# A row softmax on one core: row maxima leave the main path, ten tiles become five, and one queue carries every transfer

## The chip, the cores and the metric

The kernel runs on one core of a Trainium2 chip. The metric is the device time of one execution in microseconds (us), the median of several runs.

## The reference, cut to what matters

```python
# x: (16, 1024, 512) float32, drawn from a standard normal distribution
x_scaled = x / 2.0
x_max = np.max(x_scaled, axis=-1, keepdims=True)
exp_x = np.exp(x_scaled - x_max)
return (exp_x / np.sum(exp_x, axis=-1, keepdims=True)).astype(np.float32)
```

Each of the 16,384 rows of 512 numbers is normalised on its own. Subtracting the row maximum leaves the quotient as it is as long as neither the exponentials nor their sum leave the range of float32.

## The kernel before

Spread over 128 partitions, the 16,384 rows are 128 rows for each partition, and "a row" below means one row in every partition: 128 x 512 floats, 262,144 bytes. The table PLAN cuts the 128 rows into ten tiles of 3, 7, 13 and seven times 15 rows. A tile is what one load and one store move. In DRAM, the rows of a tile that belong to one partition lie next to each other, so a tile of 15 rows moves 30,720 contiguous bytes for each partition. Tiles are cut further into chunks of 3 to 5 rows, 27 in all, which is what the engines work on.

The data lies in one SBUF buffer, `arena`, with room for 98 of the 128 rows. Each tile is computed in place. The last two tiles (8 and 9) reuse the places of tiles 0 to 3, so their loads (L190) must wait until the stores of those tiles have landed.

For each chunk the work passes through three steps:

- VectorE takes the negated row maxima into `stats` (`reduce_max`, L118). It first waits for the tile's load.
- ScalarE computes exp(0.5 x + bias) with the negated maximum as bias, one `activation` per row, and writes the sum of the row over the maximum in `stats` (L176 in straight code, L211 in a loop). The bias is the maximum of the unscaled row, a different shift from that of the reference; the quotient is the same.
- VectorE takes the reciprocal of the sums (L127) and multiplies the chunk by it: as one broadcast multiply over the chunk for tiles 1 to 3 (L131), as one multiply for each row in the other tiles (L138).

VectorE's order is written by hand: the maximum of chunk k stands before the reciprocal and multiply of chunk k - 2 (LAG is 2). ScalarE's order is straight code for tiles 0 to 5. For tiles 6 to 9 it is a loop over chunks of 5 rows (L201 to L220) with addresses taken from a register. The loop waits at L203 on a semaphore `s_go` that TensorE's sequencer raises for it (L168), since TensorE has nothing else to do.

There are two transfer queues. SyncE's queue issues the load of tile 0 and then all ten stores in order, each once the last multiply of its tile is done (L158). ScalarE's queue issues all other loads: tile 1 in three pieces (L110), tiles 2 to 7 (L114), and tiles 8 and 9 (L190) from within the straight code of its exponentials. The first loads are moved ahead of the barrier at the program's start. The program ends when SyncE has seen the last stores land (L162).

Of the kernel before, what the change touches and what calls it, by code (L numbers as in the profile page):

```python
# [6 lines left out]

PLAN = [
    ([3], 0), ([4, 3], 3), ([5, 4, 4], 10), ([5] * 3, 23), ([5] * 3, 38), ([5] * 3, 53),
    ([5] * 3, 68), ([5] * 3, 83), ([5] * 3, 0), ([5] * 3, 15),
]
ARENA = 98
LAG = 2

SPREAD = 1

AFTER = {8: 4, 9: 5}  # L20

FUSED = {1, 2, 3}

LOOP = 6
E = 5


@with_exitstack
def kernel(
# [5 lines left out]
    nc = tc.nc  # L35
    tc.close()
    tc.compile()
    fp32 = mybir.dt.float32

    xf = x.flatten_outer_dims()  # L40
    of = out.flatten_outer_dims()
    N, D = xf.shape
    P = nc.NUM_PARTITIONS
    n_rows = N // P
    assert sum(sum(c) for c, _ in PLAN) == n_rows

    arena = nc.alloc_sbuf_tensor("arena", (P, ARENA, D), fp32)

    stats = nc.alloc_sbuf_tensor("stats", (P, n_rows), fp32)
    recip = nc.alloc_sbuf_tensor("recip", (P, n_rows), fp32)  # L50

    tiles, chunks, base = [], [], 0
    for t, (cs, at) in enumerate(PLAN):
        r = sum(cs)
        tiles.append((base, r, at))
        o = 0
        for c in cs:
            chunks.append((t, base + o, c, at + o))  # L60
            o += c
        base += r
    last_chunk = {c[0]: k for k, c in enumerate(chunks)}

    def dram(ap, t):
        b, r, _ = tiles[t]
        return ap[b * P : (b + r) * P].rearrange("(p r) d -> p r d", r=r)

    def sb(t):
        _, r, at = tiles[t]  # L70
        return arena[:, at : at + r, :]


    behind = {}
    for t, (_, r, at) in enumerate(tiles):
        for u in range(t):
            _, ru, au = tiles[u]
            if at < au + ru and au < at + r:
                behind.setdefault(t, []).append(u)

    ld = [nc.alloc_semaphore(f"ld{t}") for t in range(len(tiles))]
    awaited = sorted({u for us in behind.values() for u in us})


    st, need = {}, {}
    for t in sorted(behind):
        new = [u for u in behind[t] if u not in st]
        sem = nc.alloc_semaphore(f"st{t}")
        st.update({u: sem for u in new})
        need[t] = (sem, 16 * len(new))  # L90
    s_end = nc.alloc_semaphore("s_end")
    s_max = nc.alloc_semaphore("s_max")
    s_exp = nc.alloc_semaphore("s_exp")
    s_go = nc.alloc_semaphore("s_go")
    s_rec = nc.alloc_semaphore("s_rec")
    s_mul = nc.alloc_semaphore("s_mul")

    def issue_loads(begin, end):


        for t in range(begin, end):
            if t in behind:
                continue
            if t == 0:
                nc.sync.dma_start(out=sb(t), in_=dram(xf, t)).then_inc(ld[t], 16)
            elif t == SPREAD:

                r = tiles[t][1] - 1
                for p, q, lo, hi in ((0, P, 0, r), (0, 126, r, r + 1), (126, P, r, r + 1)):
                    nc.scalar.dma_start(  # L110
                        out=sb(t)[p:q, lo:hi], in_=dram(xf, t)[p:q, lo:hi]
                    ).then_inc(ld[t], 16)
            else:
                nc.scalar.dma_start(out=sb(t), in_=dram(xf, t)).then_inc(ld[t], 16)  # L114

    def do_max(k):
        t, b, c, a = chunks[k]
        nc.vector.reduce_max(  # L118
            out=stats[:, b : b + c],
            in_=arena[:, a : a + c],  # L120
            axis=mybir.AxisListType.X,
            negate=True,
        )._wait_ge(ld[t], 48 if t == SPREAD else 16).then_inc(s_max, 1)

    def do_mul(k):
        t, b, c, a = chunks[k]
        nc.vector.reciprocal(  # L127
            out=recip[:, b : b + c], in_=stats[:, b : b + c]
        )._wait_ge(s_exp, k + 1).then_inc(s_rec, 1)
        if t in FUSED:  # L130
            nc.vector.tensor_mul(  # L131
                out=arena[:, a : a + c],
                in0=arena[:, a : a + c],
                in1=recip[:, b : b + c].unsqueeze(2).to_broadcast([P, c, D]),
            )._wait_ge(s_rec, k + 1).then_inc(s_mul, 1)
            return
        for r in range(c):
            ins = nc.vector.tensor_scalar_mul(  # L138
                out=arena[:, a + r],
                in0=arena[:, a + r],  # L140
                scalar1=recip[:, b + r : b + r + 1],
            )
            if r == 0:
                ins._wait_ge(s_rec, k + 1)
        ins.then_inc(s_mul, 1)

    def compute_and_store():

        for k in range(len(chunks) + LAG):
            if k < len(chunks):  # L150
                do_max(k)
            if k >= LAG:
                do_mul(k - LAG)


        for t in range(len(tiles)):
            nc.sync.wait_ge(s_mul, last_chunk[t] + 1)
            nc.sync.dma_start(out=dram(of, t), in_=sb(t)).then_inc(  # L158
                st[t] if t in awaited else s_end, 16
            )  # L160

        nc.sync.wait_ge(s_end, 16 * (len(tiles) - len(awaited)))  # L162


        straight = [k for k, c in enumerate(chunks) if c[0] < LOOP]
        loop = [k for k, c in enumerate(chunks) if c[0] >= LOOP]
        for k in loop:
            nc.tensor.wait_ge(s_max, k + 1).then_inc(s_go, 1)  # L168


        nc.scalar.preload_act_table(mybir.ActivationFunctionType.Exp)  # L171
        late = sorted(behind)
        for k in straight:
            t, b, c, a = chunks[k]
            for r in range(c):
                ins = nc.scalar.activation(  # L176
                    out=arena[:, a + r],
                    in_=arena[:, a + r],
                    func=mybir.ActivationFunctionType.Exp,
                    bias=stats[:, b + r : b + r + 1],  # L180
                    scale=0.5,
                    accum_out=stats[:, b + r : b + r + 1],
                )
                if r == 0:
                    ins._wait_ge(s_max, k + 1)
            ins.then_inc(s_exp, 1)
            while late and last_chunk[AFTER[late[0]]] <= k:
                u = late.pop(0)
                nc.scalar.wait_ge(*need[u])
                nc.scalar.dma_start(out=sb(u), in_=dram(xf, u)).then_inc(ld[u], 16)  # L190
        assert not late


        first = chunks[loop[0]][1]
        assert all(
            c == E and b == first + j * E and a == b % ARENA
            for j, (_, b, c, a) in enumerate(chunks[k] for k in loop)
        )
        row = nc.scalar.alloc_register("row")
        nc.scalar.reg_mov(row, first)  # L200
        with nc.scalar.While(lambda: nc.scalar.snap(row, min_val=first, max_val=n_rows) < n_rows):  # L201
            now = nc.scalar.snap(row, min_val=first, max_val=n_rows - E)
            nc.scalar.wait_ge(s_go, 1).then_inc(s_go, -1)  # L203
            at = nc.s_assert_within(
                now % ARENA, 0, ARENA - E,
                skip_runtime_bounds_check_because="no chunk reaches over the arena's end",
            )
            for r in range(E):
                data = arena[:, r : ARENA - E + 1 + r][:, bass.ds(at, 1)]
                stat = stats[:, r : n_rows - E + 1 + r][:, bass.ds(now, 1)]  # L210
                ins = nc.scalar.activation(  # L211
                    out=data,
                    in_=data,
                    func=mybir.ActivationFunctionType.Exp,
                    bias=stat,
                    scale=0.5,
                    accum_out=stat,
                )
            ins.then_inc(s_exp, 1)
            nc.scalar.reg_add(row, row, E)  # L220

    here = str(nc.cur_bb)
    entry, rest = nc.main_func.blocks[0], list(nc.main_func.blocks[1:])
    head, jumps = entry.instructions[:-5], entry.instructions[-5:]
    entry.instructions = []
    nc.switch_bb("main", None)
    issue_loads(0, 2)
    first = list(entry.instructions)  # L230
    at = next(k for k, i in enumerate(head) if type(i).__name__ == "InstDrain")
    entry.instructions = head[:at] + first + head[at:]
    act = []
    entry.instructions = list(entry.instructions) + [i for i in jumps if i not in act]
    nc.switch_body(here, parent=None, valid_engines=[i.engine for i in jumps])
    issue_loads(2, len(tiles))
    compute_and_store()


# [28 lines left out]
```

## Time and profile before

| what | value |
|---|---|
| median of 3 runs | 160.08 us (160.05 to 160.23) |
| profiled execution, its own time | 160.0 us |
| its span in the profile | 158.6 us |
| VectorE busy | 131.4 us, 83% of the span |
| ScalarE busy | 94.4 us, 60% of the span |
| TensorE | only waits and signals, no busy time |
| read from and written to HBM | 33.55 MB each, 423 GB/s over the span |
| transfer packets | 3026, of them 336 under 2 KB |

The span is the time from the first to the last instruction that the profiler recorded; the execution's own time is 1.4 us longer. The page counts an engine as busy only while it computes. The row "DMA" is the mean busy share of the core's 16 transfer engines in each of 40 equal slices of the span, and "GB/s" is what they moved in that slice. Queue q1 is SyncE's and q10 is ScalarE's; q14 fetches instructions. "ACTq" and "SPq" are the sequencers of ScalarE and SyncE, which handle registers, branches, waits and transfer issues; "ACT" and "DVE" are the engines ScalarE and VectorE.

### The profile page before, as it was taken

Reading aid. Unit: us, or ns where it says so; the run is one execution under the profiler, and the core shown is the slowest. Engines: PE = TensorE matmul, PEld = TensorE weight load, DVE = VectorE, ACT = ScalarE, POOL = GpSimd, SP = SyncE. Lnnn points to the kernel's source line nnn. Section 1 sums busy time; section 2 is a strip of 40 time slices with the busy share of each in tenths; the row PEclk is TensorE's granted clock in tenths of the full one; section 3 lists DMA queues with packets and bytes.
Section 4 is the critical chain, followed back from the end, with each engine's and each line's share of the span. In section 5 each row is a group of like instructions: output and inputs, shape, how many; then the busy total and the mean of one; then the engine's idle time right before and its main releaser. Section 6 shows DMA issues by size and latency. Waiting matters only on the chain.

```text
span 158.6 us, 621 instructions
## 1 busy us (share of the span) xinstructions
DVE 131.4 (83%) x155; ACT 94.4 (60%) x257; POOL 0.2 (0%) x4
## 2 busy tenths in 40 slices
DVE  0466799999999999999999999996999389999000
ACT  0369197736874594669738797666566809763000
POOL 0000000000000000000000000000000000000000
DMA  7999999999999999999999999999999999999996
GB/s 268 449 373 430 414 431 466 435 407 399 466 443 389 434 463 448 418 444 426 442 426 434 426 426 442 426 441 411 457 395 472 395 473 395 472 395 465 395 472 263
DMA packets 3026, 67.13 MB, mean 423 GB/s; under 512 B 336, under 2 KB 336, under 8 KB 720
## 3 DMA queue, kind: packets, MB, share of 16 engines
q1 hardware_dynamic: 1584, 34.34, 50.6%
q10 hardware_dynamic: 1440, 32.77, 48.5%
q14 instruction: 2, 0.02, 0.0%
HBM read 33.55 MB, written 33.55 MB: 423 GB/s over the span
## 4 chain that ended last, share of the span: by engine, by line
DMA 52%; DVE 38%; issue 0%
DMA arena<-in_x_dram 38%; DVE stats L118 18%; DMA out_dram<-arena 14%; DVE arena L131 13%; DVE arena L138 7%; DVE recip L127 1%
## 5 line engine op out<-in xcount | busy, mean ns | idle before, releaser
L118 DVE TENSOR_REDUCE stats<-arena 128x5 f32<-128x2560 f32 (+2 forms) x27 | 72.2, 2676 | 14.6 <-DMA arena<-in_x_dram 14.6
L176 ACT ACTIVATE arena<-arena,stats 128x512 f32<-128x512 f32 x68 | 48.2, 710 | 23.4 <-DVE stats L118 23.4
L211 ACT ACTIVATE arena<-arena,stats x60 | 42.5, 710 | 20.7 <-ACTq L203 20.7
L138 DVE TENSOR_SCALAR arena<-arena,recip 128x512 f32<-128x512 f32 x93 | 38.6, 482 | 0.7
L131 DVE TENSOR_TENSOR arena<-arena,recip 128x2560 f32<-128x2560 f32 (+2 forms) x8 | 19.9, 2491 | 0.3
L176 ACT ACTIVATION_READ_ACCUMULATOR arena<-arena,stats 128x1 f32 x68 | 12.7, 187 | 0.0
L211 ACT ACTIVATION_READ_ACCUMULATOR arena<-arena,stats x60 | 11.2, 187 | 0.0
L127 DVE RECIPROCAL recip<-stats 128x5 f32<-128x5 f32 (+2 forms) x27 | 4.8, 177 | 0.0
L171 ACT ACT_TABLE_LOAD x1 | 1.3, 1283 | 5.7 <-issue 5.7
L252 POOL MEMSET const-bfloat16-1.0<- 128x1 bf16 x1 | 0.1, 101 | 0.0
L252 POOL MEMSET const-uint8-127<- 128x1 uint8 x1 | 0.1, 101 | 0.0
L252 POOL MEMSET const-float32-0.0<- 128x1 f32 x1 | 0.1, 98 | 0.2 <-issue 0.2
L252 POOL MEMSET const-float32-1.0<- 128x1 f32 x1 | 0.1, 98 | 0.0
## 6 DMA issues: line engine op xcount, KB each, us to landing
arena<-in_x_dram ACTq DMA_DIRECT2D x7, 3840.0 KB, 46.6
out_dram<-arena SPq DMA_DIRECT2D x7, 3840.0 KB, 22.7
arena<-in_x_dram ACTq DMA_DIRECT2D x1, 3328.0 KB, 14.3
out_dram<-arena SPq DMA_DIRECT2D x1, 3328.0 KB, 21.1
out_dram<-arena SPq DMA_DIRECT2D x1, 1792.0 KB, 18.2
arena<-in_x_dram ACTq DMA_DIRECT2D x1, 1536.0 KB
arena<-in_x_dram SPq DMA_DIRECT2D x1, 768.0 KB, 6.2
out_dram<-arena SPq DMA_DIRECT2D x1, 768.0 KB, 15.8
```

Source lines behind the costliest of these rows:

```text
L118: nc.vector.reduce_max(out=stats[:, b : b + c], in_=arena[:, a : a + c], axis=mybir.AxisListType.X, negate=True,)._wait_ge(ld[t], 48 if t ...
L127: nc.vector.reciprocal(out=recip[:, b : b + c], in_=stats[:, b : b + c])._wait_ge(s_exp, k + 1).then_inc(s_rec, 1)
L131: nc.vector.tensor_mul(out=arena[:, a : a + c], in0=arena[:, a : a + c], in1=recip[:, b : b + c].unsqueeze(2).to_broadcast([P, c, D]),)._w ...
L138: ins = nc.vector.tensor_scalar_mul(out=arena[:, a + r], in0=arena[:, a + r], scalar1=recip[:, b + r : b + r + 1],)
L171: nc.scalar.preload_act_table(mybir.ActivationFunctionType.Exp)
L176: ins = nc.scalar.activation(out=arena[:, a + r], in_=arena[:, a + r], func=mybir.ActivationFunctionType.Exp, bias=stats[:, b + r : b + r ...
L211: ins = nc.scalar.activation(out=data, in_=data, func=mybir.ActivationFunctionType.Exp, bias=stat, scale=0.5, accum_out=stat,)
L252: nc = _bacc.Bacc("TRN2", target_bir_lowering=False, num_devices=1)
```

## The change

The change does six things at once.

- **No row maxima on the main path.** ScalarE computes exp(0.5 x) without a bias and sums each row. VectorE only takes reciprocals and multiplies.
- **A check of the sums and a general path.** At the end VectorE counts, for each partition, the sums that lie between 1.0 and 1e30. TensorE adds the 128 counts with one matmul, and VectorE turns the total into a flag. VectorE, ScalarE and SyncE each read the flag into a register. Where it says that every sum was in range, they skip a loop; otherwise the loop does the whole softmax again in 16 tiles of 8 rows with row maxima.
- **Five tiles** of 30, 30, 30, 25 and 13 rows instead of ten. A tile of 30 rows moves 61,440 contiguous bytes for each partition. Tiles 3 and 4 reuse the place of tile 0.
- **All transfers on SyncE's queue**, in this order: load 0 (ahead of the barrier), loads 1 and 2, store 0, store 1, then a wait until store 0 has landed, loads 3 and 4, stores 2, 3 and 4. ScalarE issues none.
- **ScalarE loops from the start**: 25 rounds of 5 rows, then 3 rows in straight code. TensorE raises `s_go` when a tile's load has landed, by the number of chunks in the tile.
- **One broadcast multiply for every chunk** (25 of 5 rows, one of 3) in place of 93 multiplies of single rows and 8 broadcast ones. The hand-written alternation with the maxima is gone.

Line numbers in the changed kernel: transfers are issued at L93 (loads) and L97 (stores), reciprocals at L127, multiplies at L130, the loop's exponentials at L237 and the last three at L163, the check at L135 to L145, the matmul at L154, the reading of the flag at L110.

```diff
-PLAN = [
-    ([3], 0), ([4, 3], 3), ([5, 4, 4], 10), ([5] * 3, 23), ([5] * 3, 38), ([5] * 3, 53),
-    ([5] * 3, 68), ([5] * 3, 83), ([5] * 3, 0), ([5] * 3, 15),
-]
+TILES = [(30, 8), (30, 38), (30, 68), (25, 0), (13, 25)]
...
+    def load(eng, t):
+        eng.dma_start(out=sb(t), in_=dram(xf, t)).then_inc(ld[t], 16)
+
+    def store(t):
+        nc.sync.wait_ge(s_mul, upto[t])
+        nc.sync.dma_start(out=dram(of, t), in_=sb(t)).then_inc(
+            s_first if t == 0 else s_end, 16
+        )
+
+    def take(eng, sem, n):
+        eng.wait_ge(sem, n).then_inc(sem, -n)
+
+    def rounds(eng, body):
+        last = n_rows // G
+        i = eng.alloc_register("tile")
+        eng.wait_ge(s_flag, 1)
+        eng.reg_load(i, flag[0:1, 0:1])
+        with eng.While(lambda: eng.snap(i, min_val=0, max_val=last) < last):
+            body(eng.snap(i, min_val=0, max_val=last - 1))
+            eng.reg_add(i, i, 1)
...
+        for k, (b, c) in enumerate(zip(starts, sizes)):
+            a = (b + SHIFT) % ARENA
+            nc.vector.reciprocal(
+                out=recip[:, b : b + c], in_=stats[:, b : b + c]
+            )._wait_ge(s_exp, k + 1).then_inc(s_rec, 1)
             nc.vector.tensor_mul(
                 out=arena[:, a : a + c],
                 in0=arena[:, a : a + c],
                 in1=recip[:, b : b + c].unsqueeze(2).to_broadcast([P, c, D]),
             )._wait_ge(s_rec, k + 1).then_inc(s_mul, 1)
...
+        for t in range(len(tiles)):
+            nc.tensor.wait_ge(ld[t], 16).then_inc(s_go, owner.count(t))
+        nc.tensor.wait_ge(s_ones, 1)
+        nc.tensor.matmul(
+            total[:, :], lhsT=count[:, :], rhs=ones[:, :], start=True, stop=True
+        )._wait_ge(s_cnt, 3).then_inc(s_tot, 1)
+
+        nc.scalar.preload_act_table(Exp)
+        exponentials(0, n_rows - LAST)
...
+        store(0)
+        store(1)
+        nc.sync.wait_ge(s_first, 16)
+        load(nc.sync, 3)
+        load(nc.sync, 4)
+        for t in range(2, len(tiles)):
+            store(t)
...
+        rounds(nc.vector, vector)
+        rounds(nc.scalar, scalar)
+        rounds(nc.sync, sync)
+        nc.sync.wait_ge(s_end, 16 * (len(tiles) - 1))
...
+            take(nc.scalar, s_go, 1)
             at = nc.s_assert_within(
-                now % ARENA, 0, ARENA - E,
+                (now + SHIFT) % ARENA, 0, ARENA - E,
...
                 ins = nc.scalar.activation(
-                    out=data,
-                    in_=data,
-                    func=mybir.ActivationFunctionType.Exp,
-                    bias=stat,
-                    scale=0.5,
-                    accum_out=stat,
+                    out=data, in_=data, func=Exp, scale=0.5,
+                    accum_out=stats[:, r : n_rows - E + 1 + r][:, bass.ds(now, 1)],
                 )
```

## The prediction, made before the changed kernel ran

> **What bounds the kernel now.** I read the transfers first, since the same bytes must move after the change. The page's slices and queue rows:
>
> ```profile
> DVE  0466799999999999999999999996999389999000
> ACT  0369197736874594669738797666566809763000
> ...
> DMA  7999999999999999999999999999999999999996
> ...
> q1 hardware_dynamic: 1584, 34.34, 50.6%
> q10 hardware_dynamic: 1440, 32.77, 48.5%
> ```
>
> The transfer engines are full from the first slice to the last; the two queues add up to 99.1% of them. VectorE has three empty slices at the end and ScalarE gaps all along, so neither sets the end. Next, stretches of the span (DVE, ACT and POOL busy, clock, DMA share, GB/s): only loads, mixed, and only stores on SyncE's queue:
>
> ```profile
> 6.20:14.60 8.40, 7.04 (x7) 6.06 (x16) 0.00 (x0) 1.00 1.06 426
> 80.00:127.00 47.00, 42.64 (x63) 32.72 (x90) 0.00 (x0) 1.00 1.01 433
> 127.00:157.00 30.00, 19.11 (x33) 10.91 (x30) 0.00 (x0) 1.00 1.00 433
> ```
>
> The three rates agree: neither the direction nor the number of queues matters, and one queue alone holds 433 GB/s. So the time is transfer work plus every gap in it. The work is in the packet records: a 30,720-byte packet takes 1.138 us (median), a 26,624-byte one 0.987, 14,336 0.535, 6,144 0.234; each engine has 8 packets per full tile. Ten tiles make 8 x (7 x 1.138 + 0.987 + 0.535 + 0.234) = 77.8 us each way, 155.6 in both; the split of tile 1 and 9-ns semaphore packets bring 155.8. Engines begin between 1.0 and 1.8 us and end with the last store at 157.5 to 158.2, so some 0.7 us is lost, mostly before 10 us, where first packets run slow (0.4 to 0.8 us instead of 0.234).
>
> For the edges I read ScalarE's and VectorE's timeline. The page's groups first:
>
> ```profile
> L118 DVE TENSOR_REDUCE stats<-arena 128x5 f32<-128x2560 f32 (+2 forms) x27 | 72.2, 2676 | 14.6 <-DMA arena<-in_x_dram 14.6
> L211 ACT ACTIVATE arena<-arena,stats x60 | 42.5, 710 | 20.7 <-ACTq L203 20.7
> ```
>
> The maxima cost VectorE 72.2 us, and ScalarE's loop waits 20.7 us for them through L203. What a loop round itself costs is hidden in that wait; the sequencer's own rows show it, for the round whose activations run from 82.39 to 86.02 us:
>
> ```profile
> L220 ACTq ALU_OP  x1: 44/44/44, 83.1 to 83.1; - x1
> L201 ACTq COMPARE_BRANCH  x2: 38/42/45, 83.2 to 83.4; - x2
> L203 ACTq EVENT_SEMAPHORE  x1: 17/17/17, 86.3 to 86.3; - x1
> ```
>
> Addition and branch run at 83.1 to 83.4, with three rows still to compute. Only L203's wait held the next round, until the maximum ended at 86.15; the next activation began at 86.51, 0.36 us later. With `s_go` raised in advance a round should cost five rows and nothing more.
>
> **What the Trainium skill says.** *DMA: Bandwidth & Descriptors*, "Issuing engines are not separate DMA queues": transfers of all issuers interleave on the same 16 engines. The trace agrees: one queue gives 433 GB/s, as two do. "Where 436 GB/s comes from" has a ceiling of 435.2 GB/s; 433 stands on it, so rate can't be won. *Advanced Engine Details and Errata*, "Engine Queue Depths": ScalarE holds 8 queued instructions; the early branch agrees with a queue ahead of the engine. "Latency and other measured facts" of the first page prices a `tensor_load` at about 600 ns; no run shows it yet.
>
> **Transfer work after the change.** From 26,624 to 30,720 bytes a packet grows by 0.0369 ns a byte; I carry that on: 61,440 bytes 2.271 us, 51,200 1.893. Each way 8 x (3 x 2.271 + 1.893 + 0.987) = 77.5 us, both ways 155.1, with semaphores 155.2: 0.6 less than before. No record exceeds 30,720 bytes; bounds: -0.1 us if fixed cost per packet vanishes, +3 us if large packets run 2% slower. I take the line. The start loses the slow first packets once more, but no second queue joins; I take half of the 0.7 us back, between none and all.
>
> **Whether a gap opens.** In queue order, slowest engine, 18.17 us for 30 rows: load 0 begins at 1.8, with 0.5 for the slow first packet, and lands at 20.4; load 1 at 38.6, load 2 at 56.7; store 0 at 74.9, store 1 at 93.1, load 3 at 108.2, load 4 at 116.1, store 2 at 134.3, store 3 at 149.4, store 4 at 157.3. Fast engines are 0.7 us ahead. An issue has to come before its predecessor ends there.
>
> Compute: from landing through TensorE's signal to the first activation 0.36 (semaphore packet at 127.30, VectorE at 127.66) plus the 0.36 above: 0.7 us. Rows follow every 0.706 us; the last readout ends 0.82 after its row starts. Then 0.05 to the reciprocal, 0.22 to the multiply, 2.83 for it: 3.1 us.
> - Tile 0 starts at 21.1; 30 rows end at 42.4, multiplied at 45.5. Store 0 is wanted at 56.0.
> - Tile 1 follows at once: 60 rows end at 63.6, store 1 issued at 66.7; wanted at 74.1. **Spare 7.4.**
> - Load 3 must wait for store 0 (74.9), is issued at about 75.3 and lies behind store 1 until 93.1.
> - Tile 2 ends at 84.8, store 2 ready at 87.9; wanted at 115.4.
> - Tile 3 starts at 108.9; 25 rows end at 126.7, store 3 issued at 129.8; wanted at 133.5. **Spare 3.7**, the tightest place. In the run shown the last store was issued at 147.0, 1.4 before its predecessor's first engine finished, without a gap.
> - Tile 4 ends at 136.3, store 4 issued at 138.3; wanted at 148.7.
>
> **The parts.** Removing 72.2 us of maxima, and 93 + 8 multiplies (58.5 us) for 25 x 2.83 + 1.76 = 72.5 us, gains nothing by itself: transfers cover it. It pays for the large tiles: computing starts at 21.1 instead of 6.2 us. ScalarE keeps its 128 rows; a missing bias changes no duration I can see. The loop's added register addition runs ahead as the others do; exposed, rounds cost 4.1 to 4.2 us (rival C). Twelve load and ten store issues (0.24 to 0.66 us each) become five and five; they ran beside transfers: nothing. All ten now stand on SyncE, where an issue is held by the waits ahead of it: loads 3 and 4 by both multiplies and store 0's landing, with 18 us of store 1 as cover. The check is three small VectorE operations, a matmul, a flag: under 1 us each from the 0.18-us reciprocal upward; with 0.6 for the flag read, done before 144. SyncE's last wait ends at 157.3; without that cover it adds up to 5 us.
>
> **The sum.** From before's end: 158.2 - 0.6 - 0.3 = 157.3; forward: the same 157.3. The semaphore and the end take 0.45 (158.2 to 158.65): span 157.75. With the 1.4 us around it 159.15 against 160.0. The median was 0.08 above that execution: **159.2 us**. If none of the startup is regained and engines spread as they like, 159.7; all of it, 158.8.
>
> **Rivals.**
> - A, no change (159.8 to 160.4): packets gain nothing, long first packets lose as much at the start as two queues did. For it: only 0.9 us is expected, and before split tile 1's last row by 126 and 2 partitions, which this drops. Against: the packet line.
> - B, slower, one mechanism: **turns of direction inside one queue**, at 56.7, 93.1 and 116.1 us. Here an engine alternated loads and stores between two queues, each with packets waiting; one queue might drain at a turn. Price: 0 up to the 1.0 us between the first issue and first packet, three times: up to 162.2; I take 0.7 each, 161.3. It decides from 0.4 us a turn, which eats the 0.9 and 0.3 more. Against: mixed stretches run at 433.
> - C, slower: loop rounds are not hidden. Store 1 is issued at 27.9 + 11 t for a round of t us; at t = 4.12 that is 73.2, still in time; only beyond 4.25 does it cost, about 12 us for each us more. 4.4 gives about 161.5. Against: the branch at 83.4.
> - D, large packets 2% slower: 162.3. Nothing for it but that none was seen.
>
> **Numbers.** Forecast 0.58, A 0.15, B 0.14, C 0.06, D 0.05; the general path taken after all 0.02, hundreds of us. A measurement of this kernel tells 0.2% (0.32 us) from no change. Faster, below 159.76: 0.57; same 0.16; slower, above 160.4: 0.27. The forecast alone spans 158.8 to 159.7; to hold 8 in 10 I reach to B: 158.8 to 161.3.
>
> **What would show it.** Right: DMA slices full to the end; q1 alone near 98%, about 1,440 packets, 67.1 MB; VectorE about 78 us busy with no reduce in the main path; ScalarE rows 0.706 apart across rounds; store 1 issued near 67, store 3 near 130; the chain almost all transfers. Wrong: a slice under 9 at 57, 74, 93, 116 or 134 us (the first, third and fourth mean B, the others a late store); GB/s under 425 throughout (D); gaps between rounds near 0.5 us (C); or reduce rows at L186.

## The result, and the profile after

The changed kernel took 161.41 us (median of 4 runs, 161.00 to 161.77) against 160.06 us for the kernel before in the same measurement: a ratio of 1.0081 (95% interval 1.0056 to 1.0107). It is slower, by 1.35 us or 0.8%, which is small but clear of the scatter. The forecast was faster, 159.2 us, and the range ended at 161.3, just below the median. The profiled execution took 161.32 us, with a span of 159.8 us.

The page of the changed kernel, rows of slices, queues and groups:

```profile
DVE  0000007999999998999910000000599999500000
ACT  3000059999999989999400000003999995000000
...
DMA  7999799979999988999899999998998899999994
...
q1 hardware_dynamic: 1440, 67.11, 98.2%
q14 instruction: 1, 0.01, 0.0%
...
L237 ACT ACTIVATE arena<-arena x125 | 76.6, 614 | 52.2 <-ACTq L102 52.2
L130 DVE TENSOR_TENSOR arena<-arena,recip 128x2560 f32<-128x2560 f32 (+1 forms) x26 | 72.4, 2784 | 0.9
```

The transfer engines are again full almost everywhere, now from one queue with half as many packets. The row counts a packet whole in the slice where it begins, so with packets of 2.3 us its digits swing: it falls to 7 near 18 and 34 us, where only loads run. The 8 at 57 us, which the prediction named as a sign of rival B, can therefore not be read as a gap. ScalarE and VectorE have long idle stretches. So the time was not lost to a late store. SyncE's issues of stores 1 and 3, and the last wait in the view of waits on SyncE's queue, confirm that:

```profile
L97 SPq DMA_DIRECT2D out_dram<-arena x1: 344/344/344, 61.8 to 61.8; - x1
L97 SPq DMA_DIRECT2D out_dram<-arena x1: 344/344/344, 129.0 to 129.0; - x1
```
```profile
SPq L223 <- DMA out_dram<-arena: 20.4, 1, 20.4
```

Store 1 was issued at 61.8 and its predecessor ended at 75.5 to 76.5; store 3 at 129.0, its predecessor at 134.7 to 136.4. The last 20.4 us are a wait for transfers alone.

Where, then, did the time go? Each transfer follows its predecessor in the same queue, so the time from one landing to the next is its price on the slowest engine. Stretches of the changed kernel cut at the landings (duration, busy times of PE, PEld, DVE, ACT and POOL, clock, DMA share, GB/s), for load 1, load 2, store 0, store 1 and store 2:

```profile
21.03:39.15 18.12, 0.00 (x0) 0.00 (x0) 13.91 (x10) 17.34 (x57) 0.00 (x0) 1.00 1.01 437
39.15:58.35 19.20, 0.00 (x0) 0.00 (x0) 18.91 (x13) 19.20 (x63) 0.00 (x0) 1.00 1.00 410
58.35:76.46 18.11, 0.00 (x0) 0.00 (x0) 17.31 (x13) 17.70 (x59) 0.00 (x0) 1.00 1.00 434
76.46:94.58 18.12, 0.00 (x0) 0.00 (x0) 4.12 (x3) 1.09 (x4) 0.00 (x0) 1.00 0.98 425
...
117.63:136.38 18.75, 0.00 (x0) 0.00 (x0) 18.48 (x13) 16.25 (x54) 0.00 (x0) 1.00 0.95 411
```

All five move the same 30 rows. Three take 18.1 us, which is the packet work; load 2 takes 1.1 more and store 2 0.6 more. The packet records say more. "Loss" below is what packets take beyond the median of their size, added up and divided by the 16 engines.

- **The first packets** lose 0.88 us for an engine (0.4 to 1.6) in the changed kernel. In the kernel before, it was 0.43 us up to 4 us, and another 0.54 up to 12 us, where its two queues overlap in part.
- **The last packet of load 2**, on each of the 16 engines, begins at 54.0 to 55.0 us and takes 2.8 to 3.6 us instead of 2.267: a loss of 1.0 us. It is the packet ahead of the first store. A "turn" below is the place where the engines pass from loads to stores or back; this is the first one. The later turns, at 94 us (to loads) and 116 us (to stores), cost about 0.05 us or less.
- **An instruction fetch** at 122.08 us runs on one engine: a gap of 0.30 us and then a packet 0.40 too long. That engine, which also had the slowest first packet, ends last. But the change didn't bring fetches in: the kernel before has two, and the one at 71.28 us cost its engine 0.66 us in the same way. The page of the kernel before:

```profile
q14 instruction: 2, 0.02, 0.0%
```

For this last engine the sum is: begin 1.35, work 2 x (3 x 18.12 + 15.10 + 7.87) = 154.66, first packet 1.57, turn 1.07, fetch 0.70, together 159.35, which is its end in the trace. Against the kernel before, the mean engine ends 0.43 us later (158.18 against 157.75), and the last one is 1.17 behind the mean instead of 0.44. The 0.43 us come about as follows. The mean engine begins 0.31 us later (1.49 against 1.18), has 0.6 less packet work, and loses 0.1 less in slow packets at the start; at the turn it loses 1.0, where the kernel before loses 0.24 among its early stores, at 28 to 40 us; the rest is small. The 0.43 and the larger distance of the last engine make 1.15 of the 1.32 us between the profiled executions.

### The profile page after: what moved, and what is told of

It reads as the page before. It is cut to its first block, busy times and chain, and to the rows that moved or that the text cites. A ratio compares the mean times of both kernels' runs of the same rounds, so it can differ in the third digit from the quotient of the medians.

```text
span 159.8 us, 691 instructions
## 1 busy us (share of the span) xinstructions
PE 0.2 (0%) x2; PEld 0.1 (0%) x2; DVE 78.1 (49%) x57; ACT 80.0 (50%) x257; POOL 0.2 (0%) x4
## 5 line engine op out<-in xcount | busy, mean ns | idle before, releaser
L237 ACT ACTIVATE arena<-arena x125 | 76.6, 614 | 52.2 <-ACTq L102 52.2
L130 DVE TENSOR_TENSOR arena<-arena,recip 128x2560 f32<-128x2560 f32 (+1 forms) x26 | 72.4, 2784 | 0.9
L127 DVE RECIPROCAL recip<-stats 128x5 f32<-128x5 f32 (+1 forms) x26 | 4.9, 189 | 57.1 <-ACT arena L237 56.8
L237 ACT ACTIVATION_READ_ACCUMULATOR arena<-arena x125 | 23.4, 187 | 0.0
L163 ACT ACTIVATE arena<-arena 128x512 f32<-128x512 f32 x3 | 1.8, 621 | 0.0
L163 ACT ACTIVATION_READ_ACCUMULATOR arena<-arena 128x1 f32 x3 | 0.6, 193 | 0.0
L154 PE MATMUL total<-ones,count 128*1 128x1 f32 x2 | 0.2, 164 | 137.8 <-DVE count L142 137.8
L145 DVE TENSOR_SCALAR flag<-total 1x1 int32<-1x1 f32 x1 | 0.1, 147 | 0.3 <-PE total L154 0.3
L135 DVE TENSOR_SCALAR inside<-stats 128x128 f32<-128x128 f32 x1 | 0.2, 220 | 0.0
L154 PEld LDWEIGHTS total<-ones,count 128*1 128x1 f32 x2 | 0.1, 80 | 137.8 <-DVE count L142 137.8
```

Source lines behind the costliest of these rows:

```text
L127: nc.vector.reciprocal(out=recip[:, b : b + c], in_=stats[:, b : b + c])._wait_ge(s_exp, k + 1).then_inc(s_rec, 1)
L130: nc.vector.tensor_mul(out=arena[:, a : a + c], in0=arena[:, a : a + c], in1=recip[:, b : b + c].unsqueeze(2).to_broadcast([P, c, D]),)._w ...
L135: nc.vector.tensor_scalar(out=inside[:, :], in0=stats[:, :], scalar1=LO, scalar2=HI, op0=Alu.max, op1=Alu.min,).then_inc(s_cnt, 1)
L145: nc.vector.tensor_scalar(out=flag[:, :], in0=total[:, :], scalar1=float(N), scalar2=float(n_rows // G), op0=Alu.is_ge, op1=Alu.mult,)._wa ...
L154: nc.tensor.matmul(total[:, :], lhsT=count[:, :], rhs=ones[:, :], start=True, stop=True)._wait_ge(s_cnt, 3).then_inc(s_tot, 1)
L163: ins = nc.scalar.activation(out=arena[:, a], in_=arena[:, a], func=Exp, scale=0.5, accum_out=stats[:, b : b + 1],)
```

## The experiments

All changes are to the changed kernel unless said otherwise. Times of the kernel before on the same chips were 160.09 to 160.12.

**Is the loss before the first stores a matter of the queue?** First: loads 1 and 2 on the other queue.

```diff
-        load(nc.sync, 1)
-        load(nc.sync, 2)
+        load(nc.scalar, 1)
+        load(nc.scalar, 2)
```

> Loads 1 and 2 go on ScalarE's queue; everything else is the changed kernel. Store 0 (issued near 43) then runs beside load 2 and never waits behind it in one queue. Theory T (the turn from loads to stores inside one queue costs every transfer engine about 1.0 us, at 54 to 58 us): the slow packets there vanish, the time falls from 161.4 by about 1.0 to 160.4. Theory P (packets of 61,440 bytes are the cause, at the start and at the end of the loads, whatever the queue): slow packets stay somewhere in loads 0 and 2, the time stays within 0.3 of 161.4. Theory X (an accident of one profiled execution): the cluster is gone, and the time is unchanged.

Measured: 164.78 us, ratio 1.0289 (1.0272 to 1.0306). None of the theories had this. Load 0 now shared the engines with load 1 and landed at 36.7 instead of 21.0, so store 0 was ready only at 59.1, two us after the last load had landed at 57.1, and the engines ran dry. The first stores, starting on idle engines, lost nothing; later turns did, 0.8 us at 94 (stores to loads) and 1.05 at 117 to 122 (loads to stores). The run shows what the single queue is good for, its order; it doesn't decide between the theories. But it shows that first stores need not cost anything, and that a later turn can cost as much as the first one of the changed kernel. At 94 us all 16 engines came to the turn within 0.2 us of each other, at 54 us of the changed kernel within 1.0 us; whether that matters was not tested.

Then the reverse: the stores on the other queue, all loads left where they are.

```diff
-        exponentials(0, n_rows - LAST)
+        exponentials(0, 45)
+        store(0, nc.scalar)
+        exponentials(45, 75)
+        store(1, nc.scalar)
+        exponentials(75, n_rows - LAST)
...
-        store(0)
-        store(1)
```

> Stores 0 and 1 are issued from ScalarE's queue, after 45 and 75 rows of exponentials; all loads and the other stores stay on SyncE's. Store 0 (near 49 us) then mixes with load 2 packet by packet and no engine turns from loads to stores at once. T: no cluster near 54, time lower by about 1.0, near 160.4. If the loss comes wherever loads end or stores begin: it stays, 161.4. Load 2 lands some 8 us later, near 66, which delays the tile 2 exponentials but not store 2, wanted at 115.

Measured: 162.99 us, ratio 1.0199 (1.0159 to 1.0240). The loss moved with the first stores: 1.1 us at 47 to 51, where they now mix with load 2, and some 0.5 more later; the last engine was 2.1 behind the mean. So a second queue with large packets doesn't take the loss away. T is refuted in the form in which it blamed the single queue.

**Is it the size of the packets?** Three edits: the last load packets smaller, all packets halved, the first store packets smaller.

```diff
+    CUTS = {2: [0, 17, 30]}                    # e2: load 2 alone
+    CUTS = {0: [0, 15, 30], 1: [0, 15, 30], 2: [0, 15, 30], 3: [0, 12, 25]}   # e3: loads and stores
+    edges = [0, 3, 30] if t == 0 else [0, tiles[t][1]]                        # e7: store 0
```

> Load 2 is issued as 17 and 13 rows, so that the last load packets ahead of store 0 have 26,624 bytes instead of 61,440, as they had ahead of store 2, where the same turn cost nothing. T: the cluster near 55 stays, about 1.0 us on each engine, time 161.4. P (it is the size of the last load packet): the cluster shrinks to under 0.2 us, time about 160.5. X: no cluster, time 161.4.

> Every load and store of tiles 0 to 3 is issued as two halves of its rows, so that packets have 30,720 (or 24,576 and 26,624) bytes; one queue, same order, same rows for each tile. P: the first packets lose 0.4 us or less instead of 0.88, the cluster near 54 goes, time about 160.0. T: the first packets lose less, the cluster stays, time about 161.0. Packet work by the line of the prediction: 0.6 us more than with large packets if anything.

> The changed kernel with store 0 issued as 3 and 27 rows, so that the first stores behind load 2 have packets of 6,144 bytes. If the loss of 1.0 us at the first turn comes from the size of the first store packets: it falls to 0.3 or less, time about 160.7. If it belongs to the turn: it stays near 1.0 us at 54 to 58, time 161.3.

Measured: e2 161.23 us (ratio 1.0061, 1.0041 to 1.0082), loss before the first stores 0.94; e3 160.84 us (1.0043, 1.0027 to 1.0060), loss there 0.86, first packets 0.69; e7 161.25 us (1.0063, 1.0046 to 1.0080), loss 1.1. With packets of half the size the stretch is short enough to be seen in windows. e3, columns as above:

```profile
30.00:54.00 24.00, 0.00 (x0) 0.00 (x0) 23.62 (x17) 24.00 (x79) 0.00 (x0) 1.00 1.00 431
54.00:58.00 4.00, 0.00 (x0) 0.00 (x0) 3.95 (x3) 4.00 (x15) 0.00 (x0) 1.00 1.05 361
58.00:82.00 24.00, 0.00 (x0) 0.00 (x0) 21.81 (x15) 19.16 (x63) 0.00 (x0) 1.00 1.00 430
```

The share stays full, and the rate falls from 431 to 361 GB/s for 4 us: the engines count as busy, and move less. So a busy share can't show this loss. Packet size has little part in this loss: the cluster stands at the same time in all three. P is refuted for the turn. The 0.6 us that e3 gains are a smaller spread between engines: the last one is 0.7 us behind the mean instead of 1.2. The mean engine ends no sooner than in the changed kernel (158.29 us against 158.18), though it loses 0.2 less at the first packets and 0.1 less at the turn; a later begin and the work of twice as many packets take that back.

**Is it the computing beside it, and does each turn cost?** Two kernels of transfers alone.

```diff
+        ORDER = [("L", 1), ("L", 2), ("S", 0), ("S", 1), ("L", 3), ("L", 4), ("S", 2), ("S", 3), ("S", 4)]   # d1, after load 0
+        ORDER = [("L", 1), ("S", 0), ("L", 2), ("S", 1), ("L", 3), ("S", 2), ("L", 4), ("S", 3), ("S", 4)]   # d2, after load 0
```

> The computing is left out: the output is the input. The five loads and five stores stand in the order of the changed kernel on SyncE's queue (loads 0 to 2, stores 0 and 1, loads 3 and 4, stores 2 to 4), each store waiting for its load only. T (the turn itself): the packets that end load 2 are again about 1.0 us too slow on every engine, and the span stays within 0.5 us of 159.8. If instead the exponentials and multiplies running beside the turn cause it: no slow cluster near 54 us, and the span falls by about 1.0.

> The computing is left out here too: the output is the input. Order on the one queue: load 0, load 1, store 0, load 2, store 1, load 3, store 2, load 4, stores 3 and 4, so seven turns between loads and stores (four from loads to stores) instead of three. T with a price at every turn from loads to stores: four clusters of about 1.0 us, span about 162.8. If only the first turn of a run costs: one cluster near 37 us, span about 159.8. If a turn costs only after a long stretch of loads (three in a row): no cluster, span about 158.8.

Measured (one run each): d1 160.81 us, span 159.5, and the loss at 53.6 to 57 is there, 1.07 us. The loss needs no computing beside it. Even without any computing this order of transfers took 0.7 us longer than the whole kernel before. d2 took 161.98 us, span 160.7. Its first turn from loads to stores, at 36 to 39 us, lost 1.2 us; the next three 0.15, 0.30 and 0.1; the turns from stores to loads nothing. So in this order, too, only the first turn is dear. It is also the one behind the longest stretch of loads, two in a row where the later ones are single, and this run alone doesn't part the two. Length can't be all, however: loads 3 and 4 are the same stretch in the changed kernel, where the turn behind them cost 0.02 us, and in e1, where it cost 1.05. The later losses fell unevenly: the last engine ended 1.7 us behind the mean. The expectation that only the first turn costs came near, 0.9 us short in the span.

**First store of the run, or first turn behind a stretch of loads?** e8 stores the first 5 rows early, on the other queue; e9 adds a small store of zeros at the start.

```diff
+        exponentials(0, 15)                                          # e8
+        nc.scalar.wait_ge(s_mul, 1)
+        nc.scalar.dma_start(out=dram(of, 0)[:, 0:5], in_=sb(0)[:, 0:5]).then_inc(s_first, 16)
+        exponentials(15, n_rows - LAST)
```
```diff
+        nc.scalar.wait_ge(s_zero, 1)                                 # e9
+        nc.scalar.dma_start(out=dram(of, 4)[:, 0, 0:128], in_=zeros[:, :]).then_inc(s_pre, 16)
```

> The changed kernel with the first 5 rows of tile 0 stored early, near 31 us, from ScalarE's queue (after 15 rows of exponentials), so that the first store of the run mixes with load 1; the other 25 rows of store 0 stay behind load 2 on SyncE's queue. If the loss of 1.0 us belongs to the first store of a run, wherever it falls: it moves to 31 us, nothing is left at 54. If it belongs to the turn from loads to stores inside the queue: it stays at 54. Time 161.3 either way, or 160.4 if small mixed stores hide it, as they may do in the kernel before.

> The changed kernel with one added store of zeros: 512 bytes for each partition, from a buffer of its own, issued from ScalarE's queue at the start into a part of the output that store 4 overwrites later (it waits for it). If the loss of 1.0 us is the price of the first store of a run: nothing is left at 54 us and the time falls by 0.5 to 1.0, to about 160.6. If it is the price of the turn inside the queue, which e8 only softened because it broke the stretch of loads: it stays at 54, time 161.5.

Measured: e8 160.44 us, ratio 1.0027 (1.0014 to 1.0040), a full 1.0 us below the changed kernel. The loss moved to 29 to 38 us and was almost halved, 0.57 us; the turn behind load 2 lost 0.06. The mean engine ended at 157.75 us, as in the kernel before and 0.43 sooner than in the changed kernel, and the last one 0.68 behind it instead of 1.17: about half of the gain is a smaller spread between engines. e9 took 161.27 us (1.0074, 1.0059 to 1.0088), with 0.93 us at 54 as ever. A first store as such is therefore not what costs; a store of 512 bytes for each partition at the start changes nothing, while one of 10,240 bytes in the middle of the loads takes almost half of the loss away. The two stores differ in size and in time at once, so it is not shown which of the two matters. Why the first turn from a stretch of loads costs and later ones hardly do is left open by these runs.

**The start, and the check at the end.** e4 cuts load 0 into 3 and 27 rows; e5 leaves out the check and the general path.

```diff
+    CUTS = {0: [0, 3, 30]}                                           # e4
...
-        rounds(nc.vector, vector)                                    # e5, with the check's
-        rounds(nc.scalar, scalar)                                    # five instructions
-        rounds(nc.sync, sync)
```

> Load 0 is issued as 3 rows (6,144-byte packets, as in the kernel before) and 27 rows. If the long first packets (0.4 to 1.6 us too slow, 0.88 on the mean) are due to their size, the mean loss of the first packets falls to about 0.36 as before and the time by 0.5 to about 160.9; if the loss only moves to the first packets of the 27 rows, the time stays at 161.4. Nothing should change near 54 us.

> The check of the sums and the general path are left out (the result is the same for this input). The prediction held them to be hidden. If the instruction fetch at 122 us, which cost one transfer engine 0.7 us and made it the last, belongs to the general path's longer programs: no fetch before the end, the last engine finishes within 0.5 us of the mean, time about 160.8. If not, 161.4.

Measured: e4 160.77 us (1.0038, 1.0021 to 1.0055), first packets 0.55 instead of 0.88 us, the turn unchanged at 0.90. The time fell by 0.6 us, but the profiled execution was one of the two slowest of the eight (161.36 us) and as long as that of the changed kernel, so its trace doesn't show where the gain comes from. Nor is it shown that small packets make the first ones faster: in the ten profiled executions that start one queue with packets of 61,440 bytes, the first packets lose from 0.58 (d1) to 0.95 us (the changed kernel again, below). e5 161.05 us (1.0063, 1.0045 to 1.0081): no fetch before the end, and the last engine at 158.73 instead of 159.35. That one is still 0.8 us behind the mean, not within 0.5 as expected, and the times of e5 (160.76 to 161.42) overlap those of the changed kernel. Kernels d1, d2 and f2 (below) had no such fetch either, and their last engines ended 1.2 to 1.7 us behind the mean. So the spread between engines doesn't come from the fetch alone.

**The kernel before with one part of the change.** Row maxima and bias are taken out of the kernel before; ten tiles and two queues stay.

```diff
-            if k < len(chunks):
-                do_max(k)
...
-                    ins._wait_ge(s_max, k + 1)
+                    ins._wait_ge(ld[t], 48 if t == SPREAD else 16)
```

> The kernel before with one part of the change alone: the row maxima and the bias are left out (without a check of the sums; the result is the same for this input), ten tiles and two queues stay. The prediction held that this gains nothing by itself, since transfers cover it: 160.1, within 0.2. If ScalarE's or VectorE's lateness had held stores back before, the time would fall to 159.5 or less. ScalarE's rows should follow every 0.61 us as in the changed kernel, not every 0.706.

Measured: 160.12 us, ratio 1.0001 (0.9992 to 1.0010, 12 runs). VectorE's 72.2 us of maxima were covered in full. Its groups show the exponentials, where 710 ns became 614:

```profile
L174 ACT ACTIVATE arena<-arena 128x512 f32<-128x512 f32 x68 | 41.7, 614 | 22.1 <-DMA arena<-in_x_dram 22.1
L208 ACT ACTIVATE arena<-arena x60 | 36.8, 614 | 36.1 <-PEq L166 36.1
```

So leaving the maxima out neither gains nor loses. The order and form of the transfers alone took 0.7 us more than the kernel before in d1 (one run); that they make up all of the 1.35 us is not shown.

**The same kernel again, and the remedies together.**

> The changed kernel once more, unchanged, with a second profile. If the cluster near 54 us and the fetch near 122 us belong to the kernel they come again at the same places, with about 1.0 us on each engine and 0.7 us on one; if they were accidents they are gone or elsewhere. Time 161.4.

> The changed kernel with both remedies: the early store of 5 rows from ScalarE's queue (160.44 alone) and load 0 as 3 and 27 rows (160.77 alone, against 161.45). If the two losses are separate, they add: 160.44 - 0.6 = 159.8 to 159.9. If they overlap: 160.4.

> As the one with both remedies, and the check of the sums and the general path are left out (the result is the same for this input). The fetch at 122 us should be gone, and with it up to 0.7 us on one engine: 0.3 less than with the check, about 159.5, if that engine is the last one; the same time if not.

Measured: the changed kernel again 161.51 us (1.0072, 1.0048 to 1.0097), with the loss before the first stores at the same place (0.96 us from 54.07), 0.13 at the turn at 116 us, the first packets at 0.95, and the fetch at 122.57 on the engine that again ended last: no accidents. f1, the early store with the small first load, took 160.27 us, ratio 1.0016 (1.0008 to 1.0024, 22 runs). The two remedies bring 1.1 to 1.2 of the 1.35 us; they don't add up (159.8 to 159.9 would have been the sum), and f1 (159.99 to 160.97) can't be told from the early store alone (160.18 to 160.80). In its trace the turn behind load 2 lost 0.25 us. f2, without the check, took 160.55 us (1.0030, 1.0013 to 1.0046), not faster than f1, so the fetch's part in the time isn't shown. No version tried beats the kernel before.

## Why the prediction was wrong, by its own steps

**Right: what bounds the kernel.** Transfers set the end, and the maxima gain nothing (m1). No store was late, and the spare was larger than worked out: store 1 at 61.8, not 66.7. ScalarE's rows came every 0.613 us, not 0.706, since the missing bias does change the duration. The prediction overlooked a sentence of the Trainium skill, *ScalarE: Activation LUTs*, "What ACT_TABLE_LOAD costs", which says that each operand given as a [128,1] pointer adds about 93 ns to an ACTIVATE. The trace agrees: 706 - 613 = 93. It is off the path, and moved nothing.

**Right: the packet work.** 154.7 us by the landings against 155.2; a packet of 61,440 bytes takes 2.267 us (predicted 2.271). Loop rounds are hidden (rival C), and large packets in a stretch run at full rate (rival D).

**Wrong: no gap at the turns.** The step that failed is the sentence that neither the direction nor the number of queues matters, read from three stretches of 426 to 433 GB/s, and with it the turn that the sum put at nothing. Measured, the first turn cost every engine 1.0 us. These stretches are steady states. None contains the moment in which all 16 engines pass from a pure stretch of loads to stores; the kernel before has no such moment: its first stores have small packets, start at 18 us and mix with loads. An early store that breaks this moment up (e8) brought back 1.0 us of the time. This was rival B, with 0.14. B's time, 161.3, came true, but in part by luck, as its working holds in part only: one turn at 1.0 us, not three at 0.7. Why this turn costs stays open.

**Wrong: the start.** The term for the first packet was 0.5 us, taken from 6,144-byte packets; in the changed kernel it was 0.88 on the mean and 1.57 on the engine that mattered. That the size of the packets makes the difference isn't shown. The 0.3 us "regained" at the start was not regained: the engines lost 0.88 instead of 0.97 us in slow packets, but began 0.31 later. Rival A had this right. The 0.7 us that the prediction read as lost in the kernel before was low, too: slow packets there add up to 1.3 us an engine. The records of neighbouring packets overlap by 3 to 4 ns, so that the sum of their times, 155.8, overstates the work; the difference of 0.6 us in work came out all the same.

**Wrong: the last engine.** The prediction added nothing for spread between engines. Each engine has its own 80 packets of data, so one that loses something alone, as the 0.70 us at the fetch, ends late, and the end waits for it. The last engine was 0.44 us behind the mean before and 1.17 after. What spreads the engines is only known for this profile; the fetch is part of it, but the kernel before has fetches as well. In the sum for the last engine, the work, at 154.66, is below the forecast and the begin 0.45 earlier; first packet (+1.1), turn (+1.1) and fetch (+0.7) outweigh that.

**A slip beside the path.** Rival C's 161.5 us for rounds of 4.4 us doesn't follow from its own numbers: 12 us for each us beyond 4.25 gives about 161.0. Nothing rested on it.

## What to carry to other kernels

When transfers fill the span, look for what a change does to moments, not to rates: the first packets, the first stores after a run of loads, and an engine that loses time alone. A stretch at full rate on both sides of a turn says nothing of the turn. Let small stores begin while loads are still running, before the tiles grow: here that won back 1.0 us. A small first load won 0.6 us alone, and nothing that can be told from noise beside the early store.

## What the runs showed of the hardware that was not expected

- The first turn of all 16 transfer engines from a long stretch of loads to stores costs each about 1.0 us (0.86 to 1.2 in eight kernels that make it in one queue without a store among the loads), at every packet size tried and with no computing beside it; later turns in these kernels cost 0.3 us or less. During it the busy share stays full while the rate falls (431 to 361 GB/s in e3). In e1, where the first stores began on idle engines, later turns cost 0.8 us (to loads) and 1.05 us (to stores).
- The first packets of a run lose 0.58 to 0.95 us for an engine at 61,440 bytes on one queue (ten profiled executions), 0.69 at 30,720 (one), 0.55 to 0.67 at 6,144 (e4, f1 and f2).
- An instruction fetch of 8,192 bytes takes 0.31 us of one transfer engine, and cost that engine 0.66 to 0.70 us in all (at 71.28 us of the kernel before, at 122.08 of the changed kernel).
- Reading the flag from SBUF into a register took 0.94 to 1.02 us, where the prediction had priced it at about 0.6; the measurement decides. It was hidden as foreseen.
